# RG-LRU loop of a hybrid token mixer: another order of its steps, its tail as a ninth iteration

## The chip, the core and the metric

The kernel runs on one core of a Trainium2 chip. The core has a matrix engine (PE, its weight loads are listed as PEld), a vector engine (DVE), a scalar engine for activations (ACT), a general engine (POOL) and a queue engine (SP) that issues the DMAs. Each engine works through its own list of instructions in order and waits at semaphores for the others. The metric is device microseconds for one execution, here the median of three runs.

## The reference, cut to what matters

One layer over 512 latent tokens and 256 context tokens of width 1024: adaLN modulation, a token mixer with two branches, then a gated convolutional FFN. The change lies in the token mixer:

```
glu, xr, gt, mg = split(h @ w_in)              # h: modulated, normalised tokens
u   = dwconv31(v * sigmoid(g))                 # branch a: v, g are the halves of glu
y_a = silu(layernorm(u)) @ w_proj_conv
xr  = dwconv4(xr) + bias                       # branch b, latent and context apart
for d in 0, 1:                                 # two directions
    r, i  = sigmoid(xr @ w_r[d]), sigmoid(xr @ w_i[d])     # block-diagonal, heads of 64
    log_a = -8 * r * softplus(-lam[d])
    a, u  = exp(log_a), sqrt(1 - exp(2*log_a)) * i * xr
    h     = scan(h = a*h + u)                  # latent starts from the context's end state
rec = sum over d of h (latent tokens)
y_b = (rec * gelu(gt)) @ w_proj_lru
y   = (sigmoid(g_a) * y_a + sigmoid(g_b) * y_b) @ w_out
```

## The kernel before

Channels lie on the 128 partitions and tokens along the free axis, so 1024 channels are eight blocks `b`. A product is made of three matmuls on a high and a low part of each operand (`mm3`, L135 to L138), so a weight tile arrives by DMA as `raw`, ACT copies it into `whi` (L124) and POOL subtracts to get `wlo` (L125). `queue` (L95) lists all weight tiles in the order of use; `W(key, look=2)` (L129) converts up to two tiles past the one wanted at the place in the program where it stands, and starts the DMAs of two more. `block` (L144) is one product of 128 output channels with 512 tokens: 24 matmuls. The order of everything is the order of the code; no scheduler moves an instruction.

The RG-LRU loop (L639 to L701) runs `b` from 1 to 7. Iteration b makes xr of block b, and the gates of block b-1, and ends block b-2 with its scans. On PE it issues: xr (24 matmuls on latent tokens, 24 of 262 columns on the context), the gate product r of direction 0, a g block, the gates i of direction 0 and r of direction 1, a v block, the gate i of direction 1. `xr_act` and `xr_post` (L543, L549) are the four taps of the width-4 convolution, out of PSUM. `r_act` (L581) makes a and the squares `e2` (POOL, L589), `r_dve` (L592) and `i_dve` (L596) combine, `scans_act` (L601) takes roots on ACT, `scans` (L606) multiplies (L609) and runs three scans on DVE (L613 to L615). `fill(n)` (L535) issues n instructions of the 31-tap convolution (L503) on DVE; 224 of them are to be done before the layer norm of branch a, and `offload` (L521) does 24 taps on ACT and POOL. `ada_step` (L292) sums another layer's modulation row on DVE.

PSUM sets part of the order. `mm2` gives tiles from two buffers of 1024 columns, in turn, to xr and to the four gate products. A gate product can start when the last reader of the tile two before it is done: gate i of direction 0 after the taps have read xr (L558), gate r of direction 1 after `r_dve` of direction 0, the next xr after `r_dve` of direction 1.

After the loop (L703 to L729) come the gates of block 7, scans of blocks 6 and 7, and the eight gt blocks with their gelus (`gt_act`, two at a time); `gt_post` (L630) multiplies by rec and splits into `rgh`, `rgl`. Then a loop over eight pairs of gb and yb blocks (L757 to L766), a loop of ga blocks, the layer norm of branch a, and all that follows to the end of the FFN, which the change leaves alone but for a constant in the layer norm.

Of the kernel before, what the change touches and what calls it, by code (L numbers as in the profile page):

```python
# [14 lines left out]
D = 1024  # L15
# [22 lines left out]
def backbone_kernel(es: ExitStack, tc: tile.TileContext, x, ctxt, par, wadq, wada, win, wgate, wpc, wpl, wout,  # L38
# [117 lines left out]

    es_r = ExitStack()
# [27 lines left out]
    for b in range(1, NB):  # L185
        queue(("xr", b), win[16 + b], wb)
        queue(("gate", b - 1), wgate[b - 1], [4, 128], gate_dst)
        if b + 1 < NB:
            if b > 1:
                queue(("g", b + 1), win[9 + b], wb)  # L190
            queue(("v", b + 1), win[1 + b], wb)
    for b in range(NB):
        queue(("gt", b), win[24 + b], wb)
        if b == 1:
            queue(("gate", 7), wgate[7], [4, 128], gate_dst)
    for b in range(NB):
        queue(("gb", b), win[40 + b], wb)
        queue(("yb", b), wpl[b], wb)
# [229 lines left out]
    S.activation(out=pre, in_=mones[:, 0:1], func=AF.Tanh)  # L428
# [41 lines left out]
    decay_rates()  # L470
# [72 lines left out]
    def xr_act(b, ps):  # L543
        xw = pl.tile([128, 771], F32, tag="xw", bufs=1, name="xw")
# [36 lines left out]
    def r_act(b, d):  # L581
# [7 lines left out]
        G.tensor_mul(e2, a, a)  # L589
# [40 lines left out]
    def gt_post(bs, eng=G):  # L630
        for b in bs:
            V.tensor_mul(gts[b], gts[b], rec[:, b, :])
        for b in bs:
            split(gts[b], rgh[:, b, :], rgl[:, b, :], eng)
# [3 lines left out]
    pend = None  # L638
    for b in range(1, NB):  # L639
        w = W(("xr", b))  # L640
        if b == 1:
            ps = ps1
# [4 lines left out]
        block(ps[:, T:T + TP], w, chi, clo)
        if pend is not None:
            glu_mul(*pend)
            pend = None  # L650
        if b >= 2:
            scans(b - 2)
        fill(3)
        W(("gate", b - 1))
        gate_mm(b - 1, 0, 0)
        xw = xr_act(b, ps)
# [3 lines left out]
        if b == 1:  # L660
            tg = gate_act(psg)
        elif b + 1 < NB:
            gps = mm1("g_ps")
            block(gps, W(("g", b + 1)), Ahi, Alo)
        else:
            gt_block(0)
        xr_post(b, ps, xw)
        if b in (2, 6):
            rest()
        fill(2)  # L670
        r_dve(b - 1, 0)
# [553 lines left out]
```

## Time and profile before

| | |
|---|---|
| median of three runs | 921.95 us (921.81 to 923.25) |
| the profiled execution | 923.58 us, its span 921.5 us |
| busy: PE, PEld | 865.8 us (94%), 699.4 us (76%) |
| busy: DVE, ACT, POOL | 689.0 us (75%), 433.3 us (47%), 460.9 us (50%) |
| mean granted clock of PE | 0.963 |
| chain that ended last | PE 71%, DVE 17%, ACT 8%, issue 2% |

The profiled execution's own time is its span and 2.1 us that lie around it. Matmuls are pipelined and their durations overlap, so a busy share of PE near 1 is not PE at its peak; the distance between the starts of two blocks tells its pace. The granted clock is 1.00 at 2.4 GHz and 0.50 at 1.2 GHz. In this document the end of an iteration is marked by the tanh that follows its last gate product: 101.58 us for iteration 1, 280.70 us for iteration 7.

### The profile page before, as it was taken

The page shows a single profiled execution, that of the slowest core. Times are in us where ns is not written, and L with a number is a line of the kernel's source. Part 1 is how long each engine was busy: PE and PEld are TensorE (multiplying, and loading weights), DVE is VectorE, ACT ScalarE, POOL GpSimd, SP SyncE. Part 2 cuts the span into 40 slices and gives each one's busy share as a digit, 9 for nine tenths or more (in the row PEclk, how much of TensorE's full clock was granted, in tenths as well). Part 3 has the DMA queues.
Part 4 walks back from the last instruction along what each step waited for, and adds up shares of the span by engine and source line. Part 5 has one row for each costly group of instructions (what it writes and reads, how often), then busy time and mean ns, then how long its engine had stood idle before and what let it go on. Part 6 is the DMA issues. An engine that isn't in the chain of part 4 may idle for free.

```text
span 921.5 us, 11017 instructions
## 1 busy us (share of the span) xinstructions
PE 865.8 (94%) x4114; PEld 699.4 (76%) x4114; DVE 689.0 (75%) x950; ACT 433.3 (47%) x609; POOL 460.9 (50%) x267
## 2 busy tenths in 40 slices
PE   7997988899885999999899799999999999999997
PEld 6786877677674888888677588988888888888775
DVE  4386768877885698889888524699999898998314
ACT  4283654664556665522474235454544443435312
POOL 1227455655456469965533132245645554556910
PEclk9999989998897999999999899999999999999999
DMA  9952033303121222325254240223333333333502
GB/s 354 340 204 81 34 115 107 122 34 126 58 69 48 75 76 100 115 92 173 78 183 139 90 183 23 77 95 104 136 116 115 103 115 109 110 120 111 180 1 91
DMA packets 31396, 105.97 MB, mean 115 GB/s; under 512 B 3440, under 2 KB 3568, under 8 KB 31344
## 3 DMA queue, kind: packets, MB, share of 16 engines
q1 hardware_dynamic: 31344, 105.29, 33.2%
q8 instruction: 32, 0.52, 0.3%
q14 instruction: 20, 0.16, 0.1%
HBM read 103.17 MB, written 2.10 MB: 114 GB/s over the span
## 4 chain that ended last, share of the span: by engine, by line
PE 71%; DVE 17%; ACT 8%; issue 2%; DMA 1%; POOL 1%; DVEq 0%; SPq 0%; POOLq 0%; ACTq 0%
PE up_ps L137 8%; PE up_ps L136 8%; PE up_ps L138 8%; DVE cv L503 4%; PE gate_ps L136 2%; PE yb_ps L138 2%; PE yb_ps L136 2%; PE yb_ps L137 2%; PE gb_ps L137 2%; PE gb_ps L136 2%; PE gb_ps L138 2%; PE y_ps L137 2%; PE y_ps L136 2%; PE y_ps L138 2%; PE v_ps L136 2%
## 5 line engine op out<-in xcount | busy, mean ns | idle before, releaser
L125 POOL TENSOR_TENSOR wlo<-raw,whi 128x1024 fp32r<-128x1024 f32 x118 | 291.1, 2476 | 197.2 <-ACT whi L124 197.2
L1023 DVE SCALAR_TENSOR_TENSOR cv<-zall,P,cv 128x512 f32<-128x512 f32 x240 | 161.9, 746 | 0.2
L503 DVE SCALAR_TENSOR_TENSOR cv<-glu,P,cv 128x512 f32<-128x512 f32 x208 | 141.1, 748 | 0.0
L124 ACT ACTIVATE whi<-raw 128x1024 fp32r<-128x1024 f32 x121 | 125.4, 1051 | 16.5 <-issue 10.9
L136 PE MATMUL up_ps<-Ahi,whi 128*128 128x512 f32 (+1 forms) x352 | 131.8, 374 | 0.0
L137 PE MATMUL up_ps<-Alo,whi 128*128 128x512 f32 (+1 forms) x352 | 131.7, 374 | 0.0
L138 PE MATMUL up_ps<-Ahi,wlo 128*128 128x512 f32 (+1 forms) x352 | 131.6, 374 | 0.0
L137 PEld LDWEIGHTS up_ps<-Alo,whi 128*128 128x128 f32 x352 | 66.0, 188 | 13.3
L138 PEld LDWEIGHTS up_ps<-Ahi,wlo 128*128 128x128 f32 x352 | 66.0, 188 | 13.2
L136 PEld LDWEIGHTS up_ps<-Ahi,whi 128*128 128x128 f32 x352 | 66.0, 188 | 13.1
L1009 POOL TENSOR_TENSOR acl<-fo,ach 128x512 fp32r<-128x512 f32 x20 | 26.0, 1299 | 85.5 <-ACT ach L1006 85.5
L579 ACT ACTIVATE gate_ps<-gate_ps,P 128x768 f32<-128x768 f32 x32 | 28.0, 875 | 77.9 <-PE gate_ps L138 75.5
L1023 DVE SCALAR_TENSOR_TENSOR cv<-zall,P,cc 128x512 f32<-128x512 f32 x40 | 43.2, 1108 | 21.2 <-ACT cc L997 21.2
L995 ACT ACTIVATE zall<-up_ps 128x512 f32<-128x512 f32 x40 | 23.7, 593 | 63.6 <-PE up_ps L138 63.6
L136 PE MATMUL gate_ps<-xh,gwh 128*128 128x512 f32 x64 | 28.5, 445 | 24.6 <-DVE xc L558 22.1
L589 POOL TENSOR_TENSOR e<-a 128x768 f32<-128x768 f32 x16 | 24.0, 1497 | 51.9 <-ACT a L586 48.9
L1006 ACT ACTIVATE ach<-fo 128x512 fp32r<-128x512 f32 x20 | 12.6, 632 | 66.8 <-DVE fo L1005 66.8
L598 DVE SCALAR_TENSOR_TENSOR u<-gate_ps,xc 128x768 f32<-128x768 f32 x16 | 15.3, 957 | 36.0 <-ACT gate_ps L579 36.0
L297 DVE SCALAR_TENSOR_TENSOR ggb<-wa,sT,ggb 128x1024 f32<-128x1024 f32 (+1 forms) x35 | 39.5, 1128 | 0.4
L136 PEld LDWEIGHTS gate_ps<-xh,gwh 128*128 128x128 f32 x64 | 15.2, 237 | 30.8 <-issue 24.9
L136 PE MATMUL gt_ps<-Ahi,whi 128*128 128x512 f32 x64 | 26.2, 409 | 7.0 <-ACT ge L627 7.0
L609 DVE TENSOR_TENSOR u<-u,e 128x768 f32<-128x768 f32 x9 | 15.6, 1743 | 18.0 <-ACT e L604 18.0
(385 smaller groups left out, 2229.2 us busy)
## 6 DMA issues: line engine op xcount, KB each, us to landing
raw<-in_win_dram SPq DMA_DIRECT2D x48, 512.0 KB, 3.3
raw<-in_wup_dram SPq DMA_DIRECT2D x40, 512.0 KB, 3.4
wa<-in_wada_dram SPq DMA_DIRECT2D x24, 512.0 KB, 5.4
raw<-in_wdn_dram SPq DMA_DIRECT2D x22, 512.0 KB, 3.4
wa<-in_wadq_dram SPq DMA_DIRECT2D x16, 512.0 KB, 8.4
raw<-in_wpl_dram SPq DMA_DIRECT2D x8, 512.0 KB, 3.3
raw<-in_wpc_dram SPq DMA_DIRECT2D x8, 512.0 KB, 3.4
raw<-in_wout_dram SPq DMA_DIRECT2D x8, 512.0 KB, 3.3
```

The lines of the kernel that those rows point to most:

```text
L124: S.activation(out=flat(hl[0]), in_=flat(t), func=AF.Copy)
L125: eng.tensor_sub(flat(hl[1]), flat(t), flat(hl[0]))
L136: PE.matmul(o, lh, rh, start=first, stop=False)
L137: PE.matmul(o, lh, rl, start=False, stop=False)
L138: PE.matmul(o, ll, rh, start=False, stop=last)
L297: V.scalar_tensor_tensor(out=acc, in0=w, scalar=s, in1=acc, op0=ALU.mult, op1=ALU.add)
L503: V.scalar_tensor_tensor(out=cv[b] if k else glu[:, b, 0:T], in0=glu[:, b, k:k + T], scalar=col("dw31", 31 * b + k, 1), in1=cv[b], op0=ALU ...
L579: S.activation(out=lru[b, d, q], in_=lru[b, d, q], func=AF.Tanh, scale=0.5, bias=hb[:, i:i + 1])
L589: G.tensor_mul(e2, a, a)
L995: S.activation(out=z[:, 1:1 + GH, 1:1 + GW], in_=ps.rearrange("p (r c) -> p r c", c=GW), func=AF.Copy)
L1009: G.tensor_sub(acl[:, i, :], fo[i, 0], ach[:, i, :])
L1023: V.scalar_tensor_tensor(out=o, in0=zz[i, s][:, k // 3:k // 3 + GH, k % 3:k % 3 + GW], scalar=col("dw9", 9 * (i + FW * (1 - s)) + k, 1), i ...
```

## The change

- Loop: PE issues xr, gate r, v, gates i and r, g, gate i. On DVE the taps of xr come ahead of the scans; the multiplication in front of the scans becomes `scans_mul` and stands ahead of the taps, with four `fill` instructions on either side; `glu_mul` follows within the iteration. The g block is now that of b+2 (before: b+1), so iteration 1 has one too.
- Squares `e2` move from POOL to ACT. The scans write over u. A one-element tanh (`pre`) follows the roots, so that the table of tanh is loaded there.
- Tail: block 7's gates and the gt blocks 3 to 6 become iteration 8. gt 0 takes the place of g in iteration 6, gt 1 and gt 2 stand in iteration 7. gt 0 to 4 are copied out of PSUM (`gt_copy`), and all eight gelus run in a row after the last scan.
- gb and yb: the gb block is issued one pair ahead, the weights' queue has gb(b+1) ahead of yb(b); `fill(8)` and `fill(7)` in place of twice seven.
- Ahead of the loop: `decay_rates` is cut in two and its POOL part moves up, from behind the context's modulation to before it. The constant tile of 1/D goes; the layer norm scales by 1/D in the instructions that read the sums.

Loop and tail of the diff, with the functions that they call:

```diff
     for b in range(1, NB):
         queue(("xr", b), win[16 + b], wb)
         queue(("gate", b - 1), wgate[b - 1], [4, 128], gate_dst)
         if b + 1 < NB:
-            if b > 1:
-                queue(("g", b + 1), win[9 + b], wb)
             queue(("v", b + 1), win[1 + b], wb)
+        if b + 2 < NB:
+            queue(("g", b + 2), win[10 + b], wb)
+        if b >= 6:
+            queue(("gt", b - 6), win[18 + b], wb)
...
+    queue(("gb", 0), win[40], wb)
     for b in range(NB):
-        queue(("gb", b), win[40 + b], wb)
+        if b + 1 < NB:
+            queue(("gb", b + 1), win[41 + b], wb)
         queue(("yb", b), wpl[b], wb)
...
     for k in range(3):
         ada_step(k, wa[k], ggb)
+    decay_rates()
     firsts((2,), (2,))
...
     cvt_to(7)
-    decay_rates()
     ada_step(7, wa[7], ggb)
...
-        G.tensor_mul(e2, a, a)
+        S.activation(out=e2, in_=a, func=AF.Square)
...
+    def scans_mul(b):
+        for d in range(2):
+            (V if b == 7 else (V, G)[d]).tensor_mul(lru[b, d, 1], lru[b, d, 1], lru[b, d][1])
...
+    def gt_copy(b):
+        t = plx.tile([128, 771], F32, tag="xw", name="ge")[:, 0:T] if b == 4 else t_tile("ge")
+        S.activation(out=t, in_=gts[b], func=AF.Copy)
+        gts[b] = t
...
+    for b in range(1, NB + 1):
+        last = b == NB
+        if last:
+            gt_block(3)
+            gt_copy(3)
...
+        if b >= 2:
+            scans_act(b - 2)
+        if not last:
+            block(ps[:, T:T + TP], w, chi, clo)
+        fill(8 if last else 4)
+        if b >= 2:
+            scans_mul(b - 2)
+        W(("gate", b - 1))
+        gate_mm(b - 1, 0, 0)
+        if not last:
+            xw = xr_act(b, ps)
+        r_act(b - 1, 0)
...
+        if b + 1 < NB:
+            psv = mm1("v_ps")
+            block(psv, W(("v", b + 1)), Ahi, Alo)
+        else:
+            gt_block(1 if b < NB else 4)
+            gt_copy(1 if b < NB else 4)
+        fill(0 if last else 2 if b in (2, 6) else 4)
+        if not last:
+            xr_post(b, ps, xw, 0)
+            xc_new = xcs.pop(b)
+        r_dve(b - 1, 0)
...
+        if b >= 2:
+            scans(b - 2)
+        fill(6 if last else 2)
         gate_mm(b - 1, 0, 1)
+        if last:
+            gt_block(5)
         gate_mm(b - 1, 1, 0)
...
         i_dve(b - 1, 0)
+        if b + 1 < NB:
+            glu_mul(tg, psv, b + 1)
...
+    scans_act(7)
+    gt_block(7)
+    scans_mul(7)
+    scans(7)
+    for b in range(5):
+        gt_act(b)
...
+    gt_post(range(NB))
     offload(2)
...
+    for b in range(-1, NB):
+        if b + 1 < NB:
+            psg = mm_any("gb_ps")
+            block(psg, W(("gb", b + 1)), Ahi, Alo)
+            tn = gate_act(psg)
+        if b < 0:
+            t = tn
+            continue
+        fill(8)
         offload(2)
+        ps = mm_any("yb_ps")
         block(ps, W(("yb", b)), rgh, rgl)
```

First place: DVE in iteration 5, before, from the scans of block 3 to the gate steps of block 4 (`u<-u,e` is the multiplication, `a,u` the scans, `xw` and `xc` the taps, `cv` the 31-tap convolution, `e,gate_ps` is `r_dve`).

```order
L609 TENSOR_TENSOR u<-u,e_1514 128x768
L613 SCALAR_TENSOR_TENSOR e_1514<-a,u 128x256
L614 SCALAR_TENSOR_TENSOR rec<-a,e_1514,u 128x512
L615 SCALAR_TENSOR_TENSOR e_1578<-a,u 128x768
L503 SCALAR_TENSOR_TENSOR cv_886<-glu,P,cv_886 128x512
L503 SCALAR_TENSOR_TENSOR cv_888<-glu,P,cv_888 128x512
L503 SCALAR_TENSOR_TENSOR cv_886<-glu,P,cv_886 128x512
L551 SCALAR_TENSOR_TENSOR xw<-xr_ps,P,xw 128x770
L503 SCALAR_TENSOR_TENSOR cv_888<-glu,P,cv_888 128x512
L553 SCALAR_TENSOR_TENSOR xw<-xr_ps,P,xw 128x771
L503 SCALAR_TENSOR_TENSOR cv_886<-glu,P,cv_886 128x512
L558 SCALAR_TENSOR_TENSOR xc<-xr_ps,P,xw 128x512
```

The same stretch of DVE now, in iteration 5.

```order
L620 TENSOR_TENSOR u<-u,e_1553 128x768
L512 SCALAR_TENSOR_TENSOR cv_890<-glu,P,cv_890 128x512
L512 SCALAR_TENSOR_TENSOR cv_888<-glu,P,cv_888 128x512
L512 SCALAR_TENSOR_TENSOR cv_890<-glu,P,cv_890 128x512
L512 SCALAR_TENSOR_TENSOR glu<-glu,P,cv_888 128x512
L560 SCALAR_TENSOR_TENSOR xw<-xr_ps,P,xw 128x770
L562 SCALAR_TENSOR_TENSOR xw<-xr_ps,P,xw 128x771
L567 SCALAR_TENSOR_TENSOR xc<-xr_ps,P,xw 128x512
L567 SCALAR_TENSOR_TENSOR xc<-xr_ps,P,xw 128x256
L603 SCALAR_TENSOR_TENSOR e_1766<-e_1766,gate_ps 128x768
L625 SCALAR_TENSOR_TENSOR u<-a,u 128x256
L626 SCALAR_TENSOR_TENSOR rec<-a,u 128x512
```

The three scans have moved from ahead of the taps to behind the taps and `r_dve`; four convolution instructions stand between the multiplication and the taps, and none among the taps.

Second place: ACT at the end of the tail, before, from the roots of block 7 to the first tanh of a gb block (`whi<-raw` is a weight's conversion, `rgh` the split of the product with rec, `off_acc` a tap of `offload`).

```order
L604 ACTIVATE e_2354<-e_2354 128x768
L124 ACTIVATE whi<-raw 128x1024
L627 ACT_TABLE_LOAD
L627 ACTIVATE ge<-gt_ps 128x512 x2
L124 ACTIVATE whi<-raw 128x1024
L627 ACTIVATE sa<-gt_ps 128x512
L124 ACTIVATE whi<-raw 128x1024
L627 ACTIVATE sa<-gt_ps 128x512
L124 ACTIVATE whi<-raw 128x1024
L141 ACTIVATE rgh<-ge 128x512 x4
L627 ACTIVATE sa<-gt_ps 128x512
L141 ACTIVATE rgh<-sa 128x512 x2
```

The same end of the tail on ACT now.

```order
L614 ACTIVATE e_2486<-e_2486 128x768
L122 ACTIVATE whi<-raw 128x1024
L644 ACT_TABLE_LOAD
L644 ACTIVATE ge<-ge 128x512 x5
L644 ACTIVATE sa<-gt_ps 128x512 x3
L139 ACTIVATE rgh<-ge 128x512 x5
L139 ACTIVATE rgh<-sa 128x512 x3
L536 ACTIVATE off_acc<-glu,P 128x512 x2
L122 ACTIVATE whi<-raw 128x1024
L358 ACTIVATE tg<-gb_ps 128x512
```

By the queue's order the conversion ahead of the gelus is that of gb 1, and the one behind `off_acc` is that of yb 0. Before, the conversion of yb 0 was the fourth of those shown, ahead of the splits.

## Rows read from the trace of the kernel before

**Rows 1.** Windows between the markers: us, busy (instructions) by engine, granted clock, DMA.

```profile
101.58:132.28 30.70, 28.20 (x131) 22.81 (x130) 23.27 (x27) 17.12 (x19) 16.86 (x9) 0.89 0.26 94
...
190.94:221.10 30.16, 27.00 (x121) 22.27 (x120) 23.31 (x25) 17.11 (x19) 16.86 (x9) 0.89 0.27 102
...
280.70:337.45 56.75, 46.64 (x192) 37.29 (x193) 38.92 (x38) 34.23 (x42) 28.39 (x14) 0.88 0.22 74
337.45:421.94 84.49, 84.49 (x363) 67.88 (x362) 75.48 (x114) 38.80 (x52) 73.19 (x44) 1.00 0.29 95
```

**Rows 2.** Waits of PE, iterations 2 to 7: us in total, times, longest.

```profile
PE gate_ps L136 <- DVE xc L558: 17.6, 6, 3.2
```

**Rows 3.** Chain of waits, iteration 5: start, us, what.

```profile
193.54 1.28 ACT L604
...
195.72 1.99 DVE u L609
...
197.72 2.22 DVE e L613
...
202.91 1.96 DVE cv L503 x3
...
208.61 0.49 DVE xc L558
...
221.10 0.88 ACT gate_ps L579
```

**Rows 4.** Timeline of POOL, iteration 5: start, us, what, idle before.

```profile
194.47 2.41 POOL L125 TENSOR_TENSOR wlo<-raw,whi 128x1024 fp32r<-128x1024 f32 x1
196.83 2.55 POOL L609 TENSOR_TENSOR u<-u,e 128x768 f32<-128x768 f32 x1
202.99 1.29 POOL L616 TENSOR_TENSOR rec<-rec,e 128x512 f32<-128x512 f32 x1 [3.60 <-DVE e L615]
```

**Rows 5.** Timeline of DVE, the tail.

```profile
287.41 0.69 DVE L613 TENSOR_TENSOR_SCAN e<-a,u 128x256 f32<-128x256 f32 x1
...
312.72 1.83 DVE L609 TENSOR_TENSOR u<-u,e 128x768 f32<-128x768 f32 x2 [1.20 <-ACT e L604]
...
322.89 6.91 DVE L632 TENSOR_TENSOR ge<-ge,rec 128x512 f32<-128x512 f32 x4
...
332.14 1.28 DVE L632 TENSOR_TENSOR sa<-sa,rec 128x512 f32<-128x512 f32 x2
```

**Rows 6.** Timeline of PE, first iteration.

```profile
75.30 0.50 PE L136 MATMUL xr_ps<-Ahi,whi 128*128 128x512 f32 x1 [1.37 <-DVE glu L356]
...
80.99 0.28 PE L136 MATMUL xr_ps<-chi,whi 128*128 128x262 f32 x1
...
83.92 0.39 PE L136 MATMUL gate_ps<-xh,gwh 128*128 128x512 f32 x1
```

**Rows 7.** Groups of DVE, iterations 4 to 6: count, busy, mean ns, idle before.

```profile
L594 DVE SCALAR_TENSOR_TENSOR e<-e,gate_ps 128x768 f32<-128x768 f32 x6 | 5.7, 949 | 0.3 <-POOL e L589 0.3
```

**Rows 8.** Timeline of DVE ahead of the loop.

```profile
56.27 2.61 DVE L297 SCALAR_TENSOR_TENSOR ggb<-wa,sT,ggb 128x1024 f32<-128x1024 f32 x2
...
72.38 0.25 DVE L378 RECIPROCAL nshalf<-nshalf 128x16 f32<-128x16 f32 x1 [3.78 <-POOL nshalf L377]
```

**Rows 9.** Timeline of POOL ahead of the loop.

```profile
61.90 3.16 POOL L125 TENSOR_TENSOR wlo<-raw,whi 128x1024 fp32r<-128x1024 f32 x1 [23.58 <-ACT whi L124]
...
80.19 0.25 POOL L390 TENSOR_SCALAR nshalf<-y 128x16 f32<-128x16 f32 x1
```

**Rows 10.** Timeline of PE, the tail's wait.

```profile
293.17 0.79 PE L136 MATMUL gt_ps<-Ahi,whi 128*128 128x512 f32 x1 [7.03 <-ACT ge L627]
```

**Rows 11.** Timeline of PE, the first yb block.

```profile
337.45 0.40 PE L136 MATMUL yb_ps<-rgh,whi 128*128 128x512 f32 x1
```

**Rows 12.** Windows after the loop: columns as in rows 1.

```profile
456.00:460.00 4.00, 1.52 (x5) 0.68 (x4) 3.96 (x5) 1.90 (x3) 2.40 (x1) 1.00 0.71 239
512.00:516.00 4.00, 2.15 (x4) 1.13 (x4) 3.97 (x6) 0.00 (x0) 1.45 (x1) 0.53 0.34 116
```

More of the change, by code (lines that the diff above doesn't have):

```diff
@@ L154, in rstd_of @@
         return r
+    es_x = ExitStack()
+    plx = es_x.enter_context(tc.tile_pool(name="plx", bufs=1, side="right", reuse_waits="tile"))
     es_r = ExitStack()
@@ L633, in gt_post @@
         for b in bs:
-            split(gts[b], rgh[:, b, :], rgl[:, b, :], eng)
+            split(gts[b], rgh[:, b, :], rgl[:, b, :], G if b % 3 == 2 else V)
     xr_post(0, psA, xr_act(0, psA), 0)
     xc_split(0)
[L638 to L642, printed above, removed]
-        else:
-            ps = mm2("xr_ps")
-            block(ps[:, 0:T], w, Ahi, Alo)
+    tg = gate_act(psg)
+    for b in range(1, NB + 1):
[3 more added lines that the diff above has]
+            gt_copy(3)
+        else:
+            w = W(("xr", b))
+            if b == 1:
+                ps = ps1
+            else:
+                ps = mm2("xr_ps")
+                block(ps[:, 0:T], w, Ahi, Alo)
+        if b >= 2:
             scans_act(b - 2)
[L647 to L650, printed above, removed]
+        if not last:
+            block(ps[:, T:T + TP], w, chi, clo)
+        fill(8 if last else 4)
         if b >= 2:
-            scans(b - 2)
-        fill(3)
+            scans_mul(b - 2)
         W(("gate", b - 1))
         gate_mm(b - 1, 0, 0)
-        xw = xr_act(b, ps)
+        if not last:
+            xw = xr_act(b, ps)
         r_act(b - 1, 0)
@@ L683, in backbone_kernel @@
                 nc.sync.dma_start(out=was[k], in_=wada[1, :, k, :])
-        if b + 1 < NB:
-            psv = mm1("v_ps")
-            block(psv, W(("v", b + 1)), Ahi, Alo)
-            pend = (tg, psv, b + 1)
-        else:
-            gt_block(1)
+        if b + 2 < NB:
+            psg = mm1("g_ps")
+            block(psg, W(("g", b + 2)), Ahi, Alo)
+        else:
+            gt_block((0, 2, 6)[b - 6])
+            if not last:
+                gt_copy((0, 2)[b - 6])
         if 2 <= b <= 5:
@@ L693, in backbone_kernel @@
         else:
[L694 removed]
+            fill(3)
+        r_dve(b - 1, 1)
         fill(3)
[L696 removed]
         gate_mm(b - 1, 1, 1)
         gate_tanh(b - 1, 1, 1)
[L699 to L723 removed]
+        if not last:
+            xcs[b] = xc_new
+            xc_split(b)
+        if b + 2 < NB:
+            tg = gate_act(psg)
+        i_dve(b - 1, 1)
     scans_act(7)
[L725 to L728 removed]
+    gt_block(7)
+    scans_mul(7)
     scans(7)
+    for b in range(5):
+        gt_act(b)
     es_r.close()
@@ L798, in backbone_kernel @@
     mean = cv_tile("mean")
-    PE.matmul(mean, mones, lacc[0], start=True, stop=True)
+    PE.matmul(mean, ones, lacc[0], start=True, stop=True)
     ga_mm(3, range(4, NB))
@@ L973, in backbone_kernel @@
     es_o.close()
+    es_x.close()
     pz = es.enter_context(tc.tile_pool(name="pz", bufs=1, side="right", reuse_waits="tile"))
```

106 lines of the change are left out of this document (28 added, 78 removed).

## The prediction

> **What bounds the kernel now.** I read the windows between iterations first, then the waits of PE, then the chain of one iteration. The reader should see in the windows that a loop iteration takes about 30 us (30.16 in iteration 5) while DVE is busy for 23.3, and that the granted clock is 0.89 there but 1.00 with PE never idle in the gb/yb stage [rows 1]. From that stage comes PE's pace: 15 blocks in 84.49 us [rows 1], 5.63 us each. A context part takes 83.92 - 80.99 = 2.93 us [rows 6], and a gate product, three matmuls of 512 and three of 256 columns at the same paces, about 1.07. So an iteration is 3 x 5.63 + 2.93 + 4 x 1.07 = 24.1 us of PE at full clock. The rest is one wait, for the taps' last read `xc`, 17.6 us in six iterations, 2.9 each [rows 2], and the clock that falls after it: 0.89 means 22% of the iteration at 1.2 GHz, 6.6 us in which 3.3 us of work are lost. 24.1 + 2.9 + 3.3 = 30.3.
>
> The chain says what is late. After the last gate's tanh at 190.94 ACT converts and loads the table of roots, then DVE runs multiplication, scans, convolution and taps from 195.72 to 209.10 without a pause, then PE does gates and v until the tanh at 221.10 [rows 3]. Neither DVE nor PE is full: they take turns. Two of the DVE steps are also held up by POOL. The multiplication starts at 195.72 and ends at 197.7, 0.8 after POOL's `wlo` (194.47 + 2.41); the first scan starts at 197.72 and ends 0.6 after POOL's multiplication (196.83 + 2.55) [rows 3, 4]. With POOL still they take 0.9 and 0.69 [rows 5]. That is 1.1 + 1.5 = 2.6 us an iteration.
>
> **Ahead of the loop and iteration 1.** Before, DVE waits 3.78 us for POOL's first step of the decay rates [rows 8], and PE 1.37 us for the `glu` behind it [rows 6]. Both go. But POOL's decay steps, which from the reciprocal at 72.38 [rows 8] to 80.44 took 8.1 us [rows 9], now start when DVE is through the third `ada_step`, at 58.9 [rows 8], and the `wlo` of g 2 that began at 61.90 [rows 9] queues behind them until 67. PE then waits about 1 us in g 2, so xr of block 1 starts near 75.0, not 75.30. From there iteration 1 has no wait left: xr, context, gate, v, two gates, g, gate take 24.1, and the tanh comes at about 99.2 against 101.58, though a g block was added. Gain 2.3 us. If all 5 us of that delay reach PE, it is a loss of 1.7; if none, a gain of 3.3.
>
> **The loop, iterations 2 to 7.** The taps now need only xr_act, which needs the context part. By then v runs on PE (5.63 us), and that covers the taps of about 3 us. So PE's wait for `xc` goes. What is late next is DVE's own list. Its work was 23.3 us an iteration [rows 1]; in iterations 3 to 5 it gets 13 convolution instructions where it had 10, each 0.65 [rows 3], so 25.3 (in the other three the number grows less, but DVE waits there for `ada_cols`' product or the next square; I let these balance). The last thing PE needs of it is `r_dve` of direction 1, the reader of the buffer that the next xr takes. In my walk through one iteration, from xr's start S: context ends S + 8.6, taps end S + 13, scans S + 20, then two taps of the convolution, `i_dve`, `glu`, two `ada_step`, and `r_dve` ends at S + 26, where PE is done at S + 24.1. So DVE sets the period and PE waits about 2 us for it at each xr.
>
> To 25.3 I add 1.0: the scans now start when ACT has just converted the next xr's weight, so they meet most of one `wlo` (2.41 [rows 4]) where they met 1.5 us of a multiplication, and `r_dve` may wait a little for its square. The squares cost ACT 0.9 x 2 and free POOL; ACT was busy 17.1 of 30 [rows 1], so they are hidden, and if they weren't they would cost 1.8 an iteration. The table of tanh was loaded before too: nothing. A period of 26.3, six times, is 158 us against 280.70 - 101.58 = 179.1. Gain 21.1. Bounds: 24.1 (PE alone), gain 34.5; and 28.8, if the clock falls at each wait as it did, gain 6.
>
> On that lock of the two engines the rows show what I used: the scan ended when POOL's instruction had ended [rows 3, 4]. The Trainium skill (SBUF — State Buffer, section "Who interferes with whom") says that a DVE instruction with two SBUF inputs fully blocks against a GpSimd instruction that reads SBUF, and the trace agrees for multiplication and scan (1.1 and 1.5 us). By that rule the two `ada_step`, which read two SBUF tiles, are open to it as well, now that POOL's addition of rec and `gwl` come just before them; the sum would be 894 by the rule, 889 by the rows, and no run here shows which.
>
> **The tail.** From 280.70 to yb 0 took 56.75 us [rows 1, 11]; with yb 0 and the gb 1 that is now done earlier, 68.0. PE's work in it is 5 gt, 4 gates, gb 0, gb 1, yb 0 (one gt has gone into iteration 7): 8 x 5.63 + 4.3 = 49.3. The wait of 7.03 us behind the gelus [rows 10] goes, and so does the low clock around it (0.88 [rows 1]). But the end is now a chain of DVE and ACT. The square of block 7's first direction waits for gt 3 (5.6), its copy, two table loads (1.28 [rows 3]), two roots, a conversion, tanh, Exp, tanh, square at about 0.9: 15.3 after the marker. Then on DVE `r_dve` (0.95 [rows 7]), scans of block 6 with their lock (5), six convolution taps (3.9), and `i_dve`, three taps, `r_dve`, three taps, `i_dve`: 32. Two multiplications (1.83 [rows 5]), scans 5.3, addition 0.7: 40. Eight products with rec, 0.64 each alone and 1.7 under POOL's work [rows 5]: I take 6. At 46 the last split's copy (0.6), two `offload` taps (1.3), and only then ACT converts yb 0 (1.0) and POOL subtracts (2.4): 51.4. PE, through gt 7, gb 0 and gb 1, is done at 46 and waits 5 us. yb 0 ends at 56.6. Such a wait lowers the clock (0.53 in the window 512 to 516, where PE was busy for 2.15 of 4 us [rows 12]), so I add 2 us: 58.6. Gain 9.4. Bounds: no such wait, 16; products and scans all under POOL, 4.
>
> **After that** gb and yb are PE's alone at full pace [rows 1]; 15 convolution instructions of 0.65 and a product are 10.5 us of a pair's 11.3. DVE is done earlier, but nobody waits for it there: the mean stands behind the same ga blocks. The layer norm's edit swaps instructions of like size: nothing, at worst 0.5.
>
> **Sum.** 2.3 + 21.1 + 9.4 = 32.8. 923.58 - 32.8 = 890.8 for a profiled execution, which ran 1.6 above the median: 889 us.
>
> **Rivals.**
> 1. PE becomes the bound. If DVE's stalls behind POOL fall away (2.6 of its 23.3), its list is 22.7 and PE sets 24.3: 6 x 24.3 = 146, gain 33.3, tail 11, start 2.3: 875. For it: POOL loses 3 us of squares an iteration. Against: the scans still follow a conversion.
> 2. The clock. PE waits 2 us at each xr; before, waits of 2.9 cost 3.3 more. If it falls each time to 1.2 GHz, xr and context take 2.5 longer, DVE's taps follow, the period is 28.8, the loop gains 6.3 and the tail 7; with the start 15.6: 906. For it: rows 1. Against: 2.5 us of idle PE at 456 to 460 left the clock at 1.00 [rows 12].
> 3. `ada_step` waits behind POOL's addition of rec, 1.29 us [rows 4], or a `gwl` as long, in the four iterations that have it: 5 us, 894. This is the case that the page named above would expect. For it: the multiplication's wait. Against: the addition may be over by then.
> 4. Slower. xr's start, taps, scans, `r_dve` and the next xr are a ring through one PSUM buffer, 26 us long. If xr and context run wholly at 1.2 GHz, the ring is 8.6 longer, 34.7: 6 x 4.9 = 29 us lost, 14 gained by start and tail: 937. It turns slower from 32.2 on, that is when 70% of these 8.6 us is at the low clock in every iteration. Against: the clock was low 22% of the time at worst, with longer waits.
> 5. The wait only changes its name: r_dve in place of xc, period 29.8, tail and start used up by the yb wait. 922. Against: the rows' sum of DVE.
>
> **Chances.** Forecast (880 to 898) 0.60; first rival 0.11, second 0.12, third 0.08; slower 0.05; no change 0.04. What this kernel's measurement can tell from no change is about 0.2%, 1.8 us. Faster 0.91, same 0.04, slower 0.05. The range takes in the first three rivals, 875 to 906; beyond it lie the ring, no change, and a little on the fast side.
>
> **What would show it.** In the profile after: no wait of PE for `xc` in the loop, and waits of about 2 us for `r_dve` at xr; markers 26 us apart; DVE busy for 25 of them; the first scan still ending with POOL's `wlo`; one wait of PE of some 5 us for yb 0's `whi` and `wlo`. I am wrong if PE waits longest for something else, if the markers are 24 or 29 apart, or if gb/yb is no longer full.

## The result, and the profile after

| | before | after | ratio (95% interval) |
|---|---|---|---|
| first measurement | 922.6 us | 898.5 us (892.42 to 898.84) | 0.9725 (0.9687 to 0.9764) |
| measured again, five executions | 921.69 us | 895.57 us (894.17 to 896.08) | 0.9705 (0.9691 to 0.9718) |
| forecast | | 889 us (875 to 906) | |

The ratios, here and below, are worked out from the single executions and not from the medians; one execution of experiment 7 took 4715 us, for no reason that a profile shows, and is left out.

The profiled execution of after took 892.42 us, its span is 890.6. The end of an iteration is again the start of the tanh behind its last gate product: 102.41 us for iteration 1, 259.60 for iteration 7. The windows below have the columns of [rows 1]: iterations 2, 4 and 6 (there 2 and 5), then the tail, here with yb 0 and gb 1 in it, then the other gb and yb blocks.

```profile
102.41:127.34 24.93, 24.89 (x130) 20.26 (x128) 19.47 (x24) 18.68 (x23) 14.06 (x7) 1.00 0.33 116
153.13:179.45 26.32, 24.20 (x120) 20.17 (x120) 25.27 (x29) 18.68 (x22) 13.92 (x7) 1.00 0.33 111
205.75:234.60 28.85, 26.73 (x130) 21.71 (x130) 23.10 (x31) 19.26 (x23) 13.49 (x7) 0.94 0.19 63
259.60:317.73 58.13, 51.40 (x216) 40.27 (x215) 52.77 (x59) 42.04 (x57) 34.21 (x16) 0.97 0.25 81
317.73:390.53 72.80, 72.80 (x313) 58.52 (x312) 62.55 (x92) 28.50 (x38) 65.81 (x40) 1.00 0.33 105
```

Iteration 4 takes 26.32 us, at a clock of 1.00, where iteration 5 took 30.16 before; only iteration 6 fell to 0.94 and took 28.85. The tail takes 58.13 us for what took 68.0, and behind it PE is busy the whole 72.80 us, as in the last of [rows 1].

Next the largest waits of PE from 60 to 320 us (us in total, times, longest). They answer to [rows 2].

```profile
PE xr_ps L134 <- DVE e L603: 8.8, 5, 2.1
PE g_ps L136 <- POOL wlo L123: 5.7, 1, 5.7
PE yb_ps L134 <- ACT whi L122: 2.5, 1, 2.5
PE yb_ps L136 <- POOL wlo L123: 2.2, 1, 2.2
```

The wait for `xc` is gone, and one for `r_dve` at xr has taken its place, at half the sum: 8.8 us for 17.6. The two lines of `yb_ps` make the forecast 5 us, 4.7. The second line was forecast at about 1 us. Where its 5.7 come from is seen on PE and then on POOL ahead of the loop (start, us, what, count, and in brackets the idle time before and what ended it):

```profile
71.27 0.80 PE L136 MATMUL g_ps<-Ahi,wlo 128*128 128x512 f32 x1 [5.73 <-POOL wlo L123]
```

```profile
56.07 0.22 POOL L388 TENSOR_TENSOR nshalf<-nshalf,P 128x16 f32<-128x16 f32 x1 [5.70 <-DVE P L400]
...
57.00 1.10 POOL L391 TENSOR_SCALAR y<-shalf 128x16 f32<-128x16 f32 x1
...
68.52 0.25 POOL L399 TENSOR_SCALAR nshalf<-y 128x16 f32<-128x16 f32 x1
68.85 4.69 POOL L123 TENSOR_TENSOR wlo<-raw,whi 128x1024 fp32r<-128x1024 f32 x2
```

POOL's decay steps, 16 columns wide, begin at 56.07 and end at 68.77: 12.7 us for what took 8.1 [rows 8, 9], five of them 1.08 to 1.21 us long instead of 0.25. Only then do the two `wlo` run, and the third matmul of g 2 waits for the first of them.

The same measure on each stretch, in profiled executions. The last column is the second profile of after (896.08 us), which like before's had PE at the low clock for a part of its first 30 us. The first profile did not, and was 3.05 us ahead of before (47.17 us for 50.22) at the start of the first g block, up to where PE's work is the same in both.

| step | gain forecast | first profile | second profile |
|---|---|---|---|
| start and iteration 1 | 2.3 | -0.8 | -4.3 |
| iterations 2 to 7 | 21.1 | 21.9 | 22.0 |
| tail to the end of yb 0 | 9.4 | 9.9 | 9.7 |
| all that follows | 0 | 0.2 | 0.1 |
| sum | 32.8 | 31.2 | 27.5 |

For the loop as a whole the windows tell more than the markers do. First before, then after (iterations 2 to 7):

```profile
101.58:280.70 179.12, 160.65 (x740) 131.29 (x738) 140.63 (x158) 102.09 (x113) 101.69 (x54) 0.91 0.24 83
```

```profile
102.41:259.60 157.19, 148.43 (x741) 122.85 (x740) 143.22 (x166) 113.38 (x134) 83.52 (x42) 0.99 0.29 98
```

PE does the same matmuls (740 and 741 recorded), but was busy with them for 160.65 us at a mean clock of 0.91 and now for 148.43 at 0.99. So of the 21.9 us, 12.2 are pace and 9.7 are waits (18.5 us of idle PE before, 8.8 now).

### The profile page after: what moved, and what is told of

Same layout as the page of the kernel before. It is cut to its first block, busy times and chain, and to the rows that moved or that the text cites. A ratio compares the mean times of both kernels' runs of the same rounds, so it can differ in the third digit from the quotient of the medians.

```text
span 890.6 us, 11044 instructions
## 1 busy us (share of the span) xinstructions
PE 848.2 (95%) x4114; PEld 686.2 (77%) x4114; DVE 689.3 (77%) x952; ACT 444.9 (50%) x634; POOL 441.3 (50%) x248
## 4 chain that ended last, share of the span: by engine, by line
PE 70%; DVE 18%; ACT 5%; issue 4%; POOL 2%; DMA 1%; DVEq 0%; SPq 0%; POOLq 0%; ACTq 0%
PE up_ps L135 8%; PE up_ps L136 8%; PE up_ps L134 8%; DVE cv L512 4%; PE xr_ps L134 2%; PE xr_ps L135 2%; PE xr_ps L136 2%; DVE rec L626 2%; DVE ggb L303 2%; PE y_ps L135 2%; PE y_ps L134 2%; PE y_ps L136 2%; PE yb_ps L136 1%; PE yb_ps L135 1%; PE yb_ps L134 1%
## 5 line engine op out<-in xcount | busy, mean ns | idle before, releaser
L1017 ACT ACTIVATE ach<-fo 128x512 fp32r<-128x512 f32 x20 | 12.7, 633 | 66.9 <-DVE fo L1016 66.9
L134 PE MATMUL xr_ps<-Ahi,whi 128*128 128x512 f32 x56 | 23.2, 414 | 8.8 <-DVE e L603 8.8
L538 POOL TENSOR_TENSOR off_acc<-off_acc,off_prod 128x512 f32<-128x512 f32 x22 | 28.5, 1318 | 3.9 <-ACT off_prod L536 3.9
L136 PE MATMUL g_ps<-Ahi,wlo 128*128 128x512 f32 x56 | 23.1, 412 | 5.8 <-POOL wlo L123 5.7
L134 PE MATMUL yb_ps<-rgh,whi 128*128 128x512 f32 x64 | 25.8, 404 | 2.5 <-ACT whi L122 2.5
L1008 ACT ACTIVATE cc<-up_ps,P 128x512 f32<-128x512 f32 x40 | 27.3, 682 | 1.9 <-DVE cv L1034 1.9
L136 PE MATMUL yb_ps<-rgh,wlo 128*128 128x512 f32 x64 | 26.0, 406 | 2.2 <-POOL wlo L123 2.2
```

Source lines behind the costliest of these rows:

```text
L134: PE.matmul(o, lh, rh, start=first, stop=False)
L136: PE.matmul(o, ll, rh, start=False, stop=last)
L538: G.tensor_add(a, a, o)
L1008: S.activation(out=c, in_=ps.rearrange("p (r c) -> p r c", c=GW), func=AF.Copy, scale=col("dw9", 9 * (i + FW * (1 - s)) + 4, 1))
```

## Experiments

Times are medians; "the changed kernel" is at 895.57 us, ratio 0.9705, where it isn't said otherwise. The ratios are to the kernel before, which was run beside each (921.69 us beside experiments 1 to 4, 921.68 beside 5, 6, 8 and 9, 920.95 beside 7 and 10 to 12); the changed kernel itself was run beside 2 to 4 only.

**1. The changed kernel again.** No edit.

> The changed kernel once more, nothing altered. Its profiled execution took 892.4 us at a mean granted clock of 0.987, four others 898.3 to 898.9 at 0.979 to 0.981. Theory: the 6 us are PE work at the lower of its two clock levels: 0.007 of 890 us is 6 us, so a profile near 898 should show some 12 us more of low-clock stretches, the waits being the same ones as in the first profile. Rival: a wait that differs from run to run (a DMA that lands late); then the profile shows one longer wait of PE at the same clock. Either way the median should be 898, ratio to before 0.973.

Measured 895.57 us, profiled execution 896.08 at a clock of 0.983. The first window is the changed kernel's first profile, the second this one's, both from 14.6 to 18.0 us:

```profile
14.60:18.00 3.40, 2.99 (x48) 2.19 (x47) 1.68 (x3) 1.77 (x3) 0.34 (x2) 1.00 1.03 416
```

```profile
14.60:18.00 3.40, 3.40 (x41) 2.45 (x41) 0.69 (x1) 1.07 (x2) 0.00 (x0) 0.58 1.02 414
```

PE did 48 matmuls in the one and 41 in the other, on the same program. The waits agree within 0.1 us (g 2 5.72 us, xr 8.7 in five). Iteration 1 ends at 105.87 instead of 102.41, the loop takes 157.16 instead of 157.19. So the difference between these two profiles is pace at the start, as the theory has it. The first measurement's 898.5 had clocks of 0.979 to 0.981, for which there is no profile; where those stretches lie stays open. The second median was 3 us under the first, not 898 as I expected.

**2. Decay steps later.**

```diff
         ada_step(k, wa[k], ggb)
-    decay_rates()
...
     xc_split(0)
+    decay_rates()
```

> The call of decay_rates goes from behind the third ada_step to behind the split of xc of block 0, nothing else. Theory: POOL's 12.7 us of decay steps in front of the wlo of g 2 caused PE's wait of 5.73 us in g 2 and the low clock that follows it until 75.9 (4.6 us of work at half pace, 2.3 lost). Then both go: the tanh that ends iteration 1 comes 8 us earlier than 102.41, and the whole is 8 us faster than the changed kernel, 890 us median. Rival 1: the wlo is slow by itself, stretched by the ada_steps beside it; then half the wait stays, gain 3 to 4. Rival 2: iteration 1 catches up only on paper, since the decay steps now hold POOL when the loop wants its first wlo and xl; then the wait moves to the gate of block 0, gain 0.

Measured 894.22 us, 0.9698 (0.9685 to 0.9711): 1.4 us faster, not 8. The waits of PE, and POOL's timeline:

```profile
PE xr_ps L134 <- DVE e L602: 8.7, 5, 2.1
PE v_ps L136 <- POOL wlo L123: 4.5, 1, 4.5
```

```profile
76.39 0.23 POOL L388 TENSOR_TENSOR nshalf<-nshalf,P 128x16 f32<-128x16 f32 x1
...
83.35 7.04 POOL L123 TENSOR_TENSOR wlo<-raw,whi 128x1024 fp32r<-128x1024 f32 x3
```

The wait in g 2 is gone, so the decay steps were its cause. At the new place, with no `ada_step` beside them, they take 0.20 to 0.28 us each, 6.9 in all. But now they stand ahead of the `wlo` of v 2, and PE waits 4.5 us there. That was rival 2, at another place than it named (v 2, not the gate).

**3. yb 0 converted early.**

```diff
     for b in range(5):
         gt_act(b)
+    cvt_to(index["yb", 0])
```

> One added conversion: yb 0's weight is converted right behind the gelus of gt 0 to 4, ahead of the products with rec. Theory: PE's two waits at the start of yb 0 (2.5 us for whi, 2.2 for wlo) and half of the low-clock stretch at 311 to 315 (1.7) go; POOL's wlo meets the last scan and costs the DVE chain up to 1.7. Net 3 to 5 us faster than the changed kernel, 894 us median. Rival: the DVE chain ends the tail, not the conversion: the splits of rgl for blocks 5 to 7 come later and yb 0 waits for these instead; gain under 1.5, or a loss of 1.

Measured 892.95 us, 0.9679 (0.9663 to 0.9695): 2.6 us faster, a little under the 3 to 5. DVE's last scan and PE's waits in the tail:

```profile
301.06 3.96 DVE L627 TENSOR_TENSOR_SCAN u<-a,u 128x768 f32<-128x768 f32 x1
```

```profile
305.75 0.50 PE L134 MATMUL gb_ps<-Ahi,whi 128*128 128x512 f32 x1 [1.58 <-ACT sa L644]
...
313.38 0.50 PE L135 MATMUL yb_ps<-rgl,whi 128*128 128x512 f32 x1 [1.52 <-DVE rgl L140]
```

The waits for `whi` and `wlo` went. But the scan, 1.73 us in the changed kernel, took 3.96: it ended at 305.0, about its own length after the end of POOL's `wlo` (301.00 + 2.40). What came in place are 1.58 us for a gelu and 1.52 for `rgl`. Both theories had a part of it.

**4. Scans ahead of the taps again.**

```diff
+        if b >= 2:
+            scans(b - 2)
         if not last:
             xr_post(b, ps, xw, 0)
...
-        if b >= 2:
-            scans(b - 2)
         fill(6 if last else 2)
```

> One part undone: the scans of block b-2 stand ahead of the taps of xr again, all else as in the changed kernel (the fills too). Theory: the order is what the loop's gain comes from. The taps end 5 to 7 us later, the gate product i of direction 0 waits for the xr buffer, PE's wait for xc is back with 4 to 5 us in each of six iterations, and the ring through that buffer makes the period 30 to 31 instead of 26.2: 24 to 29 us slower, 922 to 927 us median. Rival: DVE's sum of work sets the period whatever the order; the same instructions give the same period, 0 to 2 us slower.

Measured 902.57 us, 0.9795 (0.9767 to 0.9823): 7 us slower, a quarter of what I expected and more than the rival's 2. Waits of PE and the whole loop:

```profile
PE gate_ps L134 <- DVE xc L567: 15.5, 6, 2.6
```

```profile
103.10:267.06 163.96, 148.43 (x741) 122.36 (x740) 143.22 (x169) 113.34 (x134) 86.28 (x42) 0.99 0.27 94
```

The wait for `xc` is back with 2.6 us each time, and that for `r_dve` is gone: one wait instead of the other. PE's busy time is 148.43, the same as with the scans behind; the 6.8 us are idle time alone. So the order of taps and scans, the first place that was shown of the change, is worth 7 of the loop's 22 us. Experiment 9 gives another 0.8 us of the 22 to the squares. How the rest is shared among the other parts is not shown: the new order on PE, with v ahead of three of the gates, was not run by itself.

**5. r_dve of direction 1 ahead of the ada_steps.**

```diff
         if 2 <= b <= 5:
+            r_dve(b - 1, 1)
             for k in (2 * b - 4, 2 * b - 3):
                 ada_step(k, was[k], ggb)
         else:
             fill(3)
-        r_dve(b - 1, 1)
+            r_dve(b - 1, 1)
         fill(3)
```

> In iterations 2 to 5 r_dve of direction 1 goes ahead of the two ada_steps (2.6 to 2.8 us); nothing else moves. Ring theory: PE's wait of 2.1 us at xr stands for the buffer that r_dve frees; r_dve ends 2.8 us earlier, so that wait goes, and what is left is DVE's list of 25.3 us: periods of 26.3 become 25.3 to 25.5, 3 to 4 us faster than the changed kernel. Rival, DVE's sum: the list is full and only its order changes; PE's wait reappears at another place (the taps' buffer), the periods stay at 26.3 and the time within 1 us.

Measured 884.61 us, 0.9592 (0.9577 to 0.9607): 11 us faster. Iterations 4 and 5, then the waits in the loop and the loop as a whole:

```profile
153.90:177.82 23.92, 23.92 (x121) 20.06 (x120) 23.78 (x29) 18.67 (x22) 13.55 (x7) 1.00 0.32 119
177.82:201.86 24.04, 24.04 (x121) 20.18 (x121) 23.90 (x29) 18.67 (x23) 14.22 (x7) 1.00 0.35 121
```

```profile
PE xr_ps L134 <- DVE e L603: 0.8, 1, 0.8
```

```profile
105.03:251.86 146.83, 146.04 (x741) 121.62 (x740) 138.93 (x166) 113.34 (x134) 84.84 (x42) 1.00 0.31 104
```

PE is never idle in iterations 4 and 5, and they take 24 us, the 24.1 that the prediction gave for PE alone. DVE does the same 166 instructions in the loop and is busy for 138.93 us instead of 143.22, since its scans meet POOL at other moments (in iteration 4 the first takes 1.79 us and the second 1.28, where they took 0.68 and 3.23). The theory had the wait right and the floor wrong: it left DVE's list at 25.3, but 1.5 of these were waits for POOL that went with the new order.

**6. Fewer convolution taps in the loop.**

```diff
-        fill(8 if last else 4)
+        fill(8 if last else 2)
```

> fill(4) ahead of scans_mul becomes fill(2) in iterations 1 to 7: 14 instructions of the 31-tap convolution (0.65 us each in the loop, 0.74 behind it) move into the gb/yb and ga stages. Theory: DVE's list sets the period, so it falls by 1.3 us in the iterations that wait (2 to 5), to 25.0; iterations 6 and 7 gain nothing or little: 4 to 6 us faster. Behind the loop 14 x 0.74 = 10.4 us of DVE work are added, against 7.8 us in which DVE sits idle before the mean: at most 2.6 us lost, net 2 to 5 faster than the changed kernel. Rival: the taps wait for xr_act anyway (0.6 us idle before them now), so only 0.7 of the 1.3 is won per iteration and the end gives it back: no change.

Measured 894.67 us, 0.9696 (0.9681 to 0.9711): 0.9 us faster, which is no more than one execution differs from the next. The loop, then iteration 3 here and in the changed kernel, then DVE's multiplication in iteration 4:

```profile
103.78:260.93 157.15, 148.41 (x741) 122.91 (x740) 138.41 (x154) 113.33 (x135) 84.08 (x42) 0.99 0.29 98
```

```profile
128.71:154.46 25.75, 24.17 (x120) 20.15 (x120) 23.30 (x27) 18.67 (x22) 14.40 (x7) 1.00 0.34 112
```

```profile
127.34:153.13 25.79, 24.21 (x120) 20.17 (x120) 25.25 (x29) 18.67 (x22) 13.89 (x7) 1.00 0.34 113
```

```profile
160.56 2.60 DVE L620 TENSOR_TENSOR u<-u,e 128x768 f32<-128x768 f32 x1
```

DVE has 12 instructions and 4.8 us less to do in the loop, which takes 157.15 us for 157.19. Iteration 3 is the test: DVE's list is 1.95 us shorter there, the period is 25.75 for 25.79, and DVE sits idle for 1.99 us until `xr_act` is done. In iterations 4 and 5 nothing was tested, as DVE's busy time stayed at 25.25: the multiplication now lies beside POOL's and takes 2.60 us for 1.30. This is the rival.

**7. The same taps out of the ring.**

```diff
-        fill(8 if last else 4)
+        fill(8 if last else 6)
...
-        fill(6 if last else 2)
+        fill(6 if last else 0)
```

> Two convolution instructions (1.3 us) move within the iteration, from behind the scans to ahead of the multiplication: the number per iteration stays. Ring theory: from xr's start over context, taps, r_dve, scans and ada_steps to the r_dve that frees the buffer of the next xr, the chain is 26.3 us long; the two that moved were in it, and ahead of the multiplication they lie beside PE's xr, outside it. Periods of 26.3 become 25.0 in iterations 3 to 5 and 25.8 becomes 24.5 in iteration 2: 4 to 6 us faster than the changed kernel. Rival, DVE's sum: the list is as long as before, periods stay at 26.3, no change.

Measured 892.75 us, 0.9681 (0.9665 to 0.9697): 2.8 us faster. The loop:

```profile
105.39:258.27 152.88, 147.90 (x741) 122.73 (x740) 142.93 (x167) 113.36 (x134) 87.63 (x42) 0.99 0.29 100
```

It is 4.3 us shorter with DVE's work the same (142.93 for 143.22 us). PE waits for `r_dve` three times (1.5 to 1.95 us, 5.0 in all) where it waited five times, and iterations 3 and 7 have no wait and take 23.9 us. Iteration 4 holds a stretch at the low clock and took 27.66. The rival (no change) falls; by the medians the size is under the 4 to 6 expected, by the loop within it.

**8. The kernel before with its convolution instructions behind r_dve.**

```diff
             scans(b - 2)
-        fill(3)
...
-        xr_post(b, ps, xw)
+        xr_post(b, ps, xw, 0)
...
-        fill(2)
         r_dve(b - 1, 0)
+        fill(7)
```

> The kernel before the change, with one edit: the seven convolution instructions that stand between its scans and r_dve of direction 0 (three ahead of the taps, two between them, two behind) all go behind that r_dve. Scans, squares, order of PE and tail stay as they were. The five ahead of the last tap are 3.3 us, PE's wait for xc is 2.9 an iteration. If a shorter wait is all that the loop's gain needs, the wait goes, the clock stays up (37 us of the loop are at the low level, 19 us of work lost), and the period falls from 29.9 to 25 or 26: 21 to 27 us faster than the kernel before, as much as the change won in the loop. Rival: the wait goes on under another name (r_dve of direction 1 and the next xr, since DVE idles 7 us an iteration for roots and tanhs), the clock still falls: under 8 us faster.

Measured 912.59 us, 0.9895 (0.9878 to 0.9913): 9 us faster than before, 7 of them in the loop. Waits of PE, 100 to 285 us, and the loop:

```profile
PE xr_ps L136 <- DVE e L594: 15.4, 5, 3.2
```

```profile
97.45:269.78 172.33, 154.91 (x740) 127.46 (x740) 144.20 (x158) 102.08 (x114) 104.57 (x54) 0.95 0.26 87
```

The wait for `xc` became one for `r_dve`, as long as the old one (15.4 us in five), and the clock is 0.95. This is the rival in kind, though it had put the gain under 8 us, and it is what the prediction's fifth rival said of the change: the wait only changes its name. What was won in the loop is mostly pace: PE is busy for 154.91 us instead of 160.65. To move the fillers alone did not shorten the ring.

**9. Squares back on POOL.**

```diff
-        S.activation(out=e2, in_=a, func=AF.Square)
+        G.tensor_mul(e2, a, a)
```

> One part undone: the squares e2 go from ACT back to POOL (1.46 us each there, two an iteration), all else as in the changed kernel. Theory: POOL's square comes ahead of r_dve and, queued behind the wlo of that stretch, holds r_dve of direction 0 and the scans behind it; DVE has no slack in iterations 2 to 5: periods 27.5 to 28, and 8 to 12 us slower with what the clock adds. Rival: ACT is relieved by 1.7 us an iteration and the square runs in a hole of POOL: 0 to 2 us slower or none.

Measured 899.09 us, 0.9744 (0.9722 to 0.9765): 3.5 us slower. The profile shows 0.8 of them: the loop takes 157.97 us, and in iteration 4 the ada_steps on DVE and the `gwl` on POOL held each other up:

```profile
178.27 3.49 DVE L303 SCALAR_TENSOR_TENSOR ggb<-wa,sT,ggb 128x1024 f32<-128x1024 f32 x2
```

```profile
178.42 2.27 POOL L123 TENSOR_TENSOR gwl<-raw,gwh 128x512 fp32r<-128x512 f32 x1
```

`r_dve` waited 0.26 us for its square, hardly the queue that I had feared; my 8 to 12 us were wrong, the rival's 0 to 2 nearer. The other executions had clocks down to 0.978, and the rest of the 3.5 us may lie there; it isn't shown.

**10. Decay steps in two parts.**

```diff
+    decay_rates(0)          # reciprocal, 13 of POOL's steps
     for k in range(3):
         ada_step(k, wa[k], ggb)
-    decay_rates()
...
+    decay_rates(1)          # the last 9 steps
     xr_post(0, psA, xr_act(0, psA), 0)
     xc_split(0)
```

> The decay steps of POOL in two parts, all else as in the changed kernel: 13 steps of the series (with the reciprocal) ahead of the three ada_steps, the last 10 behind the wlo of xr 1 and gwl, ahead of the split of xc of block 0, where POOL sat idle for 4.2 us when all of them stood later. Theory (queue): both waits that the steps caused, 5.7 us in g 2 and, when they were later, 4.5 us in v 2, come from a wlo queued behind them. With neither wlo behind more than a few steps, PE waits under 1.5 us between 60 and 100, the clock stays up there, and the time is 6 to 8 us under the changed kernel's. Rival: the beginning of the loop is bound elsewhere (the split of xc, the exponentials); then the gain stays at the 1 to 2 us that the later place gave.

Measured 893.72 us (889.86 to 893.99), 0.9684 (0.9663 to 0.9705): 1.9 us faster, not 6 to 8. Waits of PE, and iterations 4 and 5:

```profile
PE xr_ps L134 <- DVE e L606: 8.7, 5, 2.1
...
PE xr_ps L135 <- DVE clo L140: 1.3, 1, 1.3
```

```profile
147.79:175.63 27.84, 25.72 (x120) 21.32 (x120) 25.25 (x29) 18.67 (x22) 13.86 (x7) 0.94 0.30 104
175.63:203.49 27.86, 25.74 (x120) 21.34 (x120) 25.23 (x29) 18.67 (x22) 13.87 (x7) 0.94 0.31 105
```

Both big waits ahead of the loop are gone, the longest there is 1.3 us. Iteration 1 ends at 97.08 us: 5.3 earlier than in the first profile of the changed kernel, whose start ran at the same clock. Then iterations 4 and 5 take 27.85 us where they took 26.3, with the same waits (8.7 us in five) at a clock of 0.94, while iteration 6 takes 27.33 at 1.00. The time won is there, and some of it is lost again to pace.

**11 and 12. Together.** First the edits of 5 and 10; then also yb 0's conversion behind the first five gelus with its subtraction on DVE:

```diff
-        queue(("yb", b), wpl[b], wb)
+        queue(("yb", b), wpl[b], wb, eng=G if b else V)
...
+    cvt_to(index["yb", 0])
```

> The two edits together: r_dve of direction 1 ahead of the ada_steps, and the decay steps in two parts. If they are independent, 11.0 us (measured for the first) and 6 to 8 (the theory for the second) add up: 877 to 879 us. If an iteration 1 without its wait only hands the time to the loop's first ring: 882.

> As the one before, and yb 0's weight converted behind the first five gelus, with the subtraction on DVE (about 1.3 us for 128x1024 by the two-input instructions of this width) so that no POOL instruction lies beside the last scan (that cost 2.2 us when POOL did it: 3.96 against 1.73). If the conversion was the tail's end: PE's 2.5 and 2.2 us of waits for whi and wlo go, the DVE chain is 1.3 longer, and waits for rgl of up to 1.5 come in their place: 2 to 4 us faster than without it. If the DVE chain ends the tail anyway: within 1 us of it.

The two edits gave 879.33 us, 0.9539 (0.9513 to 0.9565): 5.3 us under experiment 5 alone. The loop takes 146.84 us there, as in experiment 5, so what the decay steps win ahead of it is not lost again in it. All three gave 875.95 us, 0.9507 (0.9486 to 0.9529), the fastest version here, 2.0% under the changed kernel by the two ratios. DVE's subtraction and PE at its tail:

```profile
283.64 1.22 DVE L123 TENSOR_TENSOR wlo<-raw,whi 128x1024 fp32r<-128x1024 f32 x1
```

```profile
294.47 0.50 PE L135 MATMUL yb_ps<-rgl,whi 128*128 128x512 f32 x1 [1.28 <-POOL rgl L140]
...
298.53 0.40 PE L134 MATMUL gb_ps<-Ahi,whi 128*128 128x512 f32 x1
```

The subtraction takes DVE 1.22 us, the scan before it stays at 1.73, and PE's one wait at yb 0 is 1.28 us for `rgl`; yb 0 ends 54.7 us after iteration 7 (243.80), 59.5 without this edit.

## Why the prediction was right, and where not

The time came within the range, 9.5 us above the forecast by the first measurement and 6.6 by the second. Step by step:

- **Start: wrong, 6.6 us of the miss.** "PE then waits about 1 us in g 2" failed: it was 5.73. The queue on POOL was the one described, but I gave the decay steps the 8.1 us that they took beside one `ada_step`, and they now ran beside five. The 4.6 us between 8.1 and 12.7 are nearly all that lies between the forecast wait and the measured one. Experiment 2 shows both halves: without the steps ahead of it the wait goes, and without the `ada_step` beside them the steps take 6.9 us. The upper bound of that step, a loss of 1.7, was still too kind: it held the delay of the `wlo` at 5 us and left out the clock behind such a wait (nine matmuls of g 2 took 3.96 us, from 71.27 to 75.23, for 2.1 at full pace). The 4.7 of wait and the 1.9 of pace are the 6.6.
- **Loop: size right, reason wrong.** 157.19 us for 158 forecast, a mean period of 26.2 for 26.3, DVE busy for 25.27 in iteration 4. The sum is partly luck: only iterations 4 and 5 took 26.3; 2 and 7 took 25.0, 3 took 25.8, and 6 took 28.85. "So DVE sets the period" doesn't hold either. Experiment 6 took 1.95 us off DVE's list in iteration 3 and the period stayed; experiment 5 kept the list of instructions and gained 10.3 us in the loop. What sets the period is the ring that the prediction had walked through and then priced by DVE's list: xr, context, `xr_act`, taps, `r_dve`, scans, `ada_step`, `r_dve`, next xr. The forecast walk ended at S + 26; here are its steps on DVE in iteration 4, for S = 155.21:

```profile
165.08 1.02 DVE L560 SCALAR_TENSOR_TENSOR xw<-xr_ps,P,xw 128x770 f32<-128x770 f32 x1 [0.59 <-ACT xw L554]
...
168.66 0.95 DVE L603 SCALAR_TENSOR_TENSOR e<-e,gate_ps 128x768 f32<-128x768 f32 x1 [0.32 <-ACT e L598]
...
170.25 3.23 DVE L626 TENSOR_TENSOR_SCAN rec<-a,u 128x512 f32<-128x512 f32 x1
...
176.35 0.94 DVE L607 SCALAR_TENSOR_TENSOR u<-gate_ps,xc 128x768 f32<-128x768 f32 x1
...
177.82 2.80 DVE L303 SCALAR_TENSOR_TENSOR ggb<-wa,sT,ggb 128x1024 f32<-128x1024 f32 x2
180.53 0.95 DVE L603 SCALAR_TENSOR_TENSOR e<-e,gate_ps 128x768 f32<-128x768 f32 x1
```

  The last `r_dve` ends at 181.48, S + 26.3. What lies in that chain counts (experiments 5 and 7); what lies ahead of the taps, beside PE's xr, counted nothing in experiment 6. That 25.3 + 1.0 came to the same number was luck: the list came to 25.27 with the locks in it, and the other 1.05 is idle time of DVE, most of it the two waits for ACT shown above (0.59 for `xr_act`, 0.32 for the square).
- **The lock.** The first scan was to end with POOL's `wlo`; it was the second (170.25 + 3.23, POOL's `wlo` from 169.65 to 172.40), the first having slipped in ahead. Its price, 1.95 us (3.23 for 1.28), the 0.4 that the multiplication still loses (1.30 for 0.9) and 0.2 of `ada_step` make what the locks cost before, 2.6 us, so nothing had to be added to the list for them. Rival 3's wait of `ada_step` exists: 2.80 us for 2.60 in experiment 5, and 3.49 beside a longer `gwl` in experiment 9. In the change it cost 0.2 us an iteration, not 1.3. The Trainium skill (SBUF — State Buffer, section "Who interferes with whom") has DVE instructions with two SBUF inputs and GpSimd instructions that read SBUF shut each other out; the trace agrees for scans, multiplication and `ada_step`, and, which I had not drawn from it, for POOL's small steps, 1.10 us beside `ada_step` for 0.25 elsewhere.
- **Tail: right.** (Its first part is iteration 8, the title's ninth; the loop runs from 1 to 8.) `r_dve` of block 7 starts 15.0 us after the marker (15.3 forecast), PE waits 4.7 (5), yb 0 ends at 58.1 (58.6). The products with rec on DVE, ACT's conversion behind the taps of `offload`, then PE's two waits:

```profile
299.45 3.09 DVE L649 TENSOR_TENSOR ge<-ge,rec 128x512 f32<-128x512 f32 x5
302.46 3.00 DVE L649 TENSOR_TENSOR sa<-sa,rec 128x512 f32<-128x512 f32 x3
```

```profile
307.25 1.04 ACT L122 ACTIVATE whi<-raw 128x1024 fp32r<-128x1024 f32 x1
```

```profile
308.35 0.50 PE L134 MATMUL yb_ps<-rgh,whi 128*128 128x512 f32 x1 [2.54 <-ACT whi L122]
...
311.22 0.79 PE L136 MATMUL yb_ps<-rgh,wlo 128*128 128x512 f32 x1 [2.15 <-POOL wlo L123]
...
317.73 0.39 PE L134 MATMUL gb_ps<-Ahi,whi 128*128 128x512 f32 x1
```

  The eight products took 6.1 us for the 6 put down, five of them 0.6 each and the last three, with POOL's split beside them, 1.0.
- **The clock.** Rival 2's period of 28.8 came once, in iteration 6 (28.85), but the low clock made only 1.5 of it (27.33 at 1.00 in experiment 10). By the rows of the whole loop the clock gave 12.2 of the 21.9 us and the waits 9.7. Of the prediction's split of an iteration, the wait of 2.9 was right (18.5 us of idle PE in six) and the 3.3 of pace too much: 160.65 us busy before and 146.04 in experiment 5 at 1.00 make it 2.4. Which part of the change keeps the clock up isn't shown: with the scans first, waits of 2.6 us leave it at 0.99; before, waits of up to 3.2 [rows 2] left it at 0.91, and as long ones in experiment 8 at 0.95.
- **After that:** nothing, as forecast (0.1 to 0.2 us).

Of the distance between 889 and the second median, 895.57, the start has 6.6 and the other steps give 1.3 back; about 1 is the allowance for a profiled execution, which here was 0.5 and not 1.6 above its median. The 3 us by which the first measurement lies above the second stay open.

## What to carry to other kernels

When two engines hand one buffer back and forth, write the ring down (who frees it, and what stands ahead of that on its engine) and count what lies in it; a busy sum near the period is no proof that the engine sets it. Move the instruction that frees the buffer ahead of everything that nobody waits for: here one line gave 11 us, half as much as the whole rewritten loop. And when work goes to an engine with room, price it beside what will run next to it at the new place, and look at who queues behind it.

## What the runs showed of the hardware

- The same waits were followed by a low clock in one profile and not in another, of kernels whose loops are alike. Iteration 4 of the changed kernel took 26.32 us at 1.00 and, in experiment 10, 27.84 at 0.94, after waits of PE of 2.1 us in both; the difference, 1.5 us, is what one such stretch cost. The Trainium skill (TensorE: Matmul & The Clock Gate, section "What's actually happening") notes that the number of slow matmuls at a kernel's start changes from run to run; the trace agrees, with 48 matmuls in one execution and 41 in another of the same kernel from 14.6 to 18.0 us (experiment 1).
- POOL instructions of 16 columns were stretched more than four times beside DVE instructions of 1024 columns, from 0.25 to 1.1 us; beside convolution instructions, whose sum lies in PSUM, they were not (0.20 to 0.28 in experiment 2). Small work isn't cheap on an engine that is held up for whole instructions.
- A shorter list on DVE can be given back at once: with two convolution instructions fewer ahead of the multiplication, it met POOL's in iteration 4 and took 2.60 us for 1.30.
